# Three tiles and three loads for the normalised values of a spatial gating unit, with their operations placed behind a product of the group ahead

## The chip, the cores and the metric

The kernel runs on one core of one Trainium2 chip. The metric is device time in microseconds (us) for one launch; lower is better. Three runs of the kernel before took 1842.79, 1843.56 and 1844.47 us, so the median is 1843.56 us. Engines are named as in the profile: PE is the matrix engine (PEld its weight loads), DVE the vector engine, ACT the scalar engine, POOL GpSimd, and SP the engine whose queue issues the transfers (DMAs).

## The reference

The reference is one step of a two-layer decoder trunk over 1024 prompt tokens and 8 sample tokens, in float32. Layer 0 is a gated linear recurrence; layer 1, "layer B" here, is a chunked MLP with spatial gating. After each comes a gated per-layer embedding. The change lies in layer B:

```
def chunk_mlp_mixer(h, w_in, ln_g, ln_b, w_sp, b_sp, w_out):
    proj = h @ w_in
    u, v, z = jnp.split(proj, 3, axis=-1)
    u = jax.nn.gelu(u)
    v = layernorm(jax.nn.gelu(v), ln_g, ln_b)
    ...
    w = jnp.where(jnp.tril(jnp.ones((c, c), dtype=bool))[None], w_sp, 0.0)
    s = jnp.einsum('gts,bnsgd->bntgd', w, vc) + b_sp.T[None, None, :, :, None]
    s = s.reshape(B, n * c, D_INNER)[:, :L]
    y = (u * s * jax.nn.silu(z)) @ w_out
    v_tail = v[:, ((L - 1) // c) * c:]
    return y, v_tail
```

The inner width is 2048, in 8 groups of 256 channels; each group has its own causal 128 x 128 matrix w_sp, applied to each of the 8 chunks of 128 prompt tokens. The normalised rows of the last chunk (v_tail) are an output.

## The kernel before

Activations lie with channels on the 128 partitions and tokens along the free axis. The 1032 tokens are cut into three column chunks, called 0, 1 and 2, of 384, 384 and 264 (the last holds the 8 sample tokens); OFF, W and NT give each chunk's start, width and number of 128-token blocks (3, 3, 2). A float32 product is made from three products of split operands (`mm3`, L234 to L236): the weights are split into a high and a low part by ACT (L150) and DVE (L151), the activations likewise.

`unit` (L478) computes two output tiles of 128 channels for all three chunks. Chunks 0 and 1 together take seven products of half size instead of eight, with weights that are sums of blocks (`ssum`, split into `shi` and `slo`); chunk 2 is a plain product (`last`, x264 in the profile). The sums of the partial results are DVE operations: L520, L532, L539, L546 and L552, with ACT's copy L516 ahead of the first. Each of them reads a PSUM bank, which PE can use again once it is read. `unit` takes two callbacks: `pre(mm, c)` ahead of a product and `out(mm, c, src)` when the result of half mm and chunk c is there.

Layer B first computes v: GELU, a transposition so that tokens lie on partitions, statistics for the layer norm (L1567), and a store to DRAM, one tensor `vraw[g]` for each group of 256 channels. Then it runs over the eight groups g. A group does, in program order:

- a unit for u with GELU (`gated`, L1705);
- a load of the whole of `vraw[g]`, 1 MB, to the tile `vn` (L1722; one buffer), and eight DVE operations L1724, one for each 128-token block, that subtract the mean and multiply by the reciprocal deviation in place;
- two small loads (L1726, L1727), two POOL operations that turn the last block into the output v_tail (L1729, L1730), and its store (L1731);
- `spatial`: a unit for z. Its `pre` multiplies vn by the group's matrix (L1680, into the PSUM tile psp), adds the bias (DVE, L1683) and multiplies by u (POOL, L1689; DVE in the last group). Its `out` makes the sigmoid of z (ACT, L1695), the product sigmoid times z (DVE, L1696, the "gating product"), the product with s (DVE, L1697), and stores the result to DRAM (L1698).

In `spatial` of groups 0 to 6 the calls of `pre` come in the order (0,0), (0,2), (1,1), (0,1), (1,0), (1,2), where the first number is the half and the second the chunk. So chunk 1 of vn is read for the last time in (0,1), chunk 0 in (1,0) and chunk 2 in (1,2), which is also the last gating product of the group. In group 7 chunk 2 comes first.

In groups 4 to 7 further DVE operations (L438 to L444) and transfers prepare sums of activations for the output projection. At the end of group 7, `first_four` uses the space of vn for four results of another product: ACT copies them there (L362), and they are stored to DRAM (L363).

The order of PE's instructions is the program's own. On the other engines and on SP the compiler orders instructions by a simulated schedule of its own; `tc.high_priority` raises instructions in it (the sums of `unit` among them), and `tc.issue_after(x)` makes the instructions of a block come after x in the queue of x's engine. Each engine, and SP with its DMA issues, works through its queue in order, so an instruction that waits holds all that stand behind it. A tile with one buffer can be loaded again only when all its readers are done.

Of the kernel before, what the change touches and what calls it, by code (L numbers as in the profile page):

```python
# [8 lines left out]
F32 = mybir.dt.float32  # L9
# [4 lines left out]
ALU = mybir.AluOpType  # L14
# [3 lines left out]
P = 128  # L18
# [8 lines left out]
DV = 256  # L27
# [14 lines left out]
OFF = (0, 384, 768)  # L42
W = (384, 384, 264)
NT = (3, 3, 2)
# [37 lines left out]
def trunk_kernel(ctx, tc, xT, st, pT, nrm, wina, lbl, gna, wouta, winb, lng, lnb, lngr, lnbr,  # L82
                 wsp, bsp, woutb, wgate, wproj, cst, msk,
                 yT, so_p, so_s, cv_p, cv_s):
    nc = tc.nc
    V, A, G, PE = nc.vector, nc.scalar, nc.gpsimd, nc.tensor
# [3 lines left out]
    def pool(stack, name, bufs=1, **kw):  # L90
        return stack.enter_context(tc.tile_pool(name=name, bufs=bufs, reuse_waits="tile", **kw))
# [122 lines left out]
    def take(*key):  # L214
        n = taken[0]
        assert order[n] == key, (order[n], key)
        load(n)
        if order[n:n + 2] == [("p", 0, 1), ("oa", 0, 0)]:
            fetch_weights(n + 1)
        else:  # L220
            load(n + 1, key[0] == "b")
        taken[0] += 1
        return loaded[n]


    last, rest = {}, {}
# [143 lines left out]
    def load_zt(zt, parts, stage, n=2, lag=0, tie=True, behind=None):  # L370


        todo = [(ozd[c][:, k0 + k:k0 + k + n, :], *(x[:, k:k + n, :] for x in zt[c, k0][:2]), W[c])
                for c, k0 in parts for k in range(0, zt[c, k0][2], n)]
        return load_list(todo, stage, lag, tie, behind)
# [50 lines left out]
    def p_in_act(l, stage, load=True):  # L426

        fh, fl = (t.rearrange("p k t -> p (k t)")[:, :2 * T].rearrange("p (k t) -> p k t", k=2)
                  for t in (hh[2], hl[2]))
        for c in CH:  # L430
            o = slice(OFF[c], OFF[c] + W[c])
            for k in range(2 if load else 0):
                load_split(fh[:, k, o], fl[:, k, o], pT[l][:, k, o], stage(W[c]))
        return ([fh[:, :, OFF[c]:OFF[c] + W[c]] for c in CH], [fl[:, :, OFF[c]:OFF[c] + W[c]] for c in CH])
# [1105 lines left out]
    vraw = [dram.tile([P, 8, DV], F32, name=f"vraw{g}") for g in range(8)]  # L1540
# [50 lines left out]
    wb2 = pool(sB, "workB2", side="right")  # L1591
    wst = wb2.tile([P, 8, P], F32, name="wst")
# [23 lines left out]
    mv = wb.tile([P, 8, 2], F32, name="mv")  # L1616
    ss_ = wb2.tile([P, MI, NS], F32, name="ss_")
    ln = {}
# [47 lines left out]
    def spatial(g, vn, us, wt, then={}, early=False):  # L1666
        bts = []
        for mm in range(2):
            bt = wb2.tile([P, P], F32, name="bt", bufs=2)
            V.scalar_tensor_tensor(bt, rw[:, g, :], lg[:, 1, 2 * g + mm:2 * g + mm + 1], bspb[:, g, :],  # L1670
                                   ALU.mult, ALU.add)
            bts.append(bt)
        ss = {}

        def pre(mm, c):
            m = 2 * g + mm
            w, nt, n0 = W[c], NT[c], OFF[c] // P
            pss = p2[0].tile([P, 3, P], F32, name="psp", tag="p2", bufs=2)
            for i in range(nt):
                PE.matmul(pss[:, i, :], vn[:, n0 + i, mm * P:(mm + 1) * P], wst[:, g, :], start=True, stop=True)  # L1680
            s = ss[mm, c] = wb2.tile([P, 384], F32, name="s", bufs=3)
            with tc.high_priority(offset=PRI):
                V.scalar_tensor_tensor(s[:, :nt * P].rearrange("p (n t) -> p n t", t=P), pss[:, :nt, :],  # L1683
                                       lg[:, 0, m:m + 1],
                                       bts[mm].rearrange("p (o t) -> p o t", o=1).broadcast_to([P, nt, P]),
                                       ALU.mult, ALU.add)
            if c == 2:
                G.tensor_copy(s[:, 256:264], ln["s"][:, m, :])
            (V if g == 7 else G).tensor_tensor(s[:, :w], s[:, :w], us[mm, c][:, :w], ALU.mult)  # L1689

        def out(mm, c, src):
            w, s = W[c], ss[mm, c]
            sg = wb2.tile([P, 384], F32, name="sg", bufs=2)
            with tc.high_priority(offset=PRI if g == 7 else 0):
                A.activation(sg[:, :w], src, AF.Sigmoid)  # L1695
                V.tensor_tensor(sg[:, :w], sg[:, :w], src, ALU.mult)  # L1696
                V.tensor_tensor(s[:, :w], s[:, :w], sg[:, :w], ALU.mult)  # L1697
            nc.sync.dma_start(ozd[c][:, 2 * g + mm, :], s[:, :w])  # L1698

        unit(wt, wide_b, wb2, out, pre, early, then)  # L1700

    def gated(us):
        def out(mm, c, src):
            us[mm, c] = wide()
            A.activation(us[mm, c][:, :W[c]], src, AF.Gelu_apprx_tanh)  # L1705
        return out

    def sums_b():

        t = stats.rearrange("p n m s -> p (n m s)")  # L1710
        t = [t[:, :384], t[:, 384:]] + [wb2.tile([P, 384], F32, name=f"mix{i}") for i in range(2)]
        yield from mix_early([(tdr[3], j, 0) for j in range(4)] + [(tdr[2], j, 8) for j in range(2)], lambda: t)
        yield

    for g in range(8):
        us = {}
        if g == 4:
            sums = sums_b()
            next(sums)
        unit(take("B", 2 * g), wide_b, wb2, gated(us), then={i: lambda: next(sums) for i in ((), (3,), (3,), (3, 7))[max(g - 4, 0)]})  # L1720
        vn = wb2.tile([P, 8, DV], F32, name="vn", bufs=1)
        nc.sync.dma_start(vn, vraw[g])  # L1722
        for n in range(8):
            V.tensor_scalar(vn[:, n, :], vn[:, n, :], mv[:, n, 0:1], ln["rstd"][:, n:n + 1], ALU.subtract, ALU.mult)  # L1724
        gb = wb2.tile([P, 2, DV], F32, name="gb", bufs=1)
        nc.sync.dma_start(gb[:, 0, :], lngr[g].partition_broadcast(P))  # L1726
        nc.sync.dma_start(gb[:, 1, :], lnbr[g].partition_broadcast(P))  # L1727
        cv = gb[:, 0, :]
        G.tensor_tensor(cv, vn[:, 7, :], cv, ALU.mult)  # L1729
        G.tensor_tensor(cv, cv, gb[:, 1, :], ALU.add)  # L1730
        nc.sync.dma_start(cv_p[:, g * DV:(g + 1) * DV], cv)  # L1731
        if g < 7:
            spatial(g, vn, us, take("B", 2 * MI + 2 * g), {3: lambda: next(sums)} if g in (4, 5) else {})
        else:

            zt = {(0, 0): (hh[0], hl[0], 8), (1, 0): (*xm[1], 4), (1, 4): (*xm[0], 4), (2, 0): (hh[2], hl[2], 8)}
            ph, pl = p_in_act(1, None, False)


            free = ws[0].tile([P, 1024], F32, name="wstg3", bufs=1)  # L1740
            zq_to = itertools.cycle([free[:, 384 * i:384 * i + 384] for i in range(2)] +
                                    [t[:, 3 * i:3 * i + 3, :].rearrange("p a b -> p (a b)") for t in (rw, bspb)
                                     for i in range(2)] + [gb.rearrange("p a b -> p (a b)")[:, :384]])
            zq = load_zt(zt, [(1, 0), (0, 0), (1, 4)],
                         lambda w: next(zq_to)[:, :w].rearrange("p (k t) -> p k t", k=1),
                         1, ZQ, False)

            def fetch(n):
                return lambda: [next(zq, None) for _ in range(n)]

            pieces = [(pT[1][:, k, OFF[c]:OFF[c] + W[c]], ph[c][:, k, :], pl[c][:, k, :], W[c]) for c in CH for k in range(2)]
            pq = load_list(pieces, lambda w: ws[0].tile([P, 512], F32, name="ssum", bufs=2)[:, :w], 2, False,
                           lambda: rest["u2"])
            place = [None]
            fillb = pple(1, ph, pl, 1, lambda c, mm: place[0](c, mm))

            def both(m, n):
                def go():
                    for _ in range(m):
                        next(pq, None)  # L1760
                    fetch(n)()
                return go

            def first_four():
                vt = wb2.tile([P, 8, DV], F32, name="vn", bufs=1).rearrange("p a b -> p (a b)")
                place[0] = lambda c, mm: vt[:, 384 * mm:384 * mm + 384]
                for _ in range(4):
                    next(fillb)
                    tk.tick()

            spatial(g, vn, us, take("B", 2 * MI + 2 * g),
                    {0: both(2, ZQ), 1: lambda: next(sums), 2: both(2, 4), 3: both(2, 8), 4: both(2, 4), 8: first_four}, True)
# [155 lines left out]
```

## Time and profile before

| | us |
|---|---|
| median of the three runs | 1843.56 |
| the profiled execution | 1848.1 |
| its span, first to last instruction | 1846.4 |
| PE busy | 1821.9 |
| DVE busy | 1363.5 |
| ACT busy | 897.8 |
| POOL busy | 379.1 |

The granted clock of PE was 0.998 of full speed over the span. The groups of layer B lie between about 1195 and 1560 us. In the profile's rows, a time at the front is the start in us from the span's start, the second number the duration; "x3" counts instructions; a bracket at the end gives the idle time of the engine before the row, and what ended it. In the table of waits the three numbers are the total in us, the count and the longest. In the table of DMAs they are the size and the median time in us from issue to landing. In rows by window they are the window, its length, the busy time (and count) of PE, PEld, DVE, ACT and POOL, then PE's granted clock, the DMA engines' busy share and GB/s. The names u, c, s, sg and stats are tiles; "u" is also the name under which the sums u2 and u4 appear, and "c" stands for c22.

### The profile page before, as it was taken

How to read it: one execution, taken by the hardware profiler on the slowest of the kernel's cores; microseconds unless marked ns; L12 is line 12 of the kernel's file. 1: busy time of each engine (PE TensorE's matmuls, PEld its weight loads, DVE VectorE, ACT ScalarE, POOL GpSimd, SP SyncE). 2: the span in 40 equal slices, each digit the busy share in tenths (PEclk: the TensorE clock that was granted, in tenths of full speed). 3: DMA queues.
4: the chain of work that ended last, by engine and by line, in shares of the span. 5: the costliest groups of instructions: out<-in, count | busy, mean ns of one | idle time of the engine just before them, and what ended most of it. 6: DMA issues, size and time to landing. Idle time of an engine off the chain costs nothing.

```text
span 1846.4 us, 37297 instructions
## 1 busy us (share of the span) xinstructions
PE 1821.9 (99%) x14545; PEld 1788.9 (97%) x14545; DVE 1363.5 (74%) x2787; ACT 897.8 (49%) x1907; POOL 379.1 (21%) x384
## 2 busy tenths in 40 slices
PE   9999999999999999999999999999999999999998
PEld 8999999999999999999999999999999999999997
DVE  7866888788878886877747655587777877877654
ACT  7533366556656655354535544433333335444442
POOL 0000011111111110000424233344454550000322
PEclk9999999999999999999999999999999999999999
DMA  6233344345444357763144433333334537953222
GB/s 221 80 122 106 105 131 138 106 155 172 150 134 138 121 175 245 249 206 106 48 157 141 140 94 92 92 107 112 109 101 152 181 117 231 304 187 97 82 92 93
DMA packets 164721, 258.06 MB, mean 140 GB/s; under 512 B 16128, under 2 KB 137024, under 8 KB 163520
## 3 DMA queue, kind: packets, MB, share of 16 engines
q1 hardware_dynamic: 164544, 255.68, 43.4%
q8 instruction: 114, 1.87, 0.4%
q14 instruction: 63, 0.52, 0.1%
HBM read 182.82 MB, written 72.80 MB: 138 GB/s over the span
## 4 chain that ended last, share of the span: by engine, by line
PE 85%; DVE 7%; DMA 3%; issue 1%; ACT 1%; POOL 1%; SPq 0%; DVEq 0%; ACTq 0%; POOLq 0%
PE ps_proj L234 21%; PE ps_proj L235 20%; PE ps_proj L236 20%; PE ps_d L234 3%; PE ps_d L236 3%; PE ps_d L235 3%; PE ps_o L234 2%; PE ps_o L235 2%; PE ps_o L236 2%; PE psp L1680 1%; PE pt_o L1048 1%; DVE wlo L151 1%; PE po L236 1%; PE po L235 1%; PE po L234 1%
## 5 line engine op out<-in xcount | busy, mean ns | idle before, releaser
L234 PE MATMUL ps_proj<-bh,whi 128*128 128x384 f32 (+1 forms) x2192 | 701.1, 320 | 3.3 <-DVE vl L230 0.8
L235 PE MATMUL ps_proj<-bl,whi 128*128 128x384 f32 (+1 forms) x2192 | 682.3, 311 | 2.0 <-DVE bl L230 1.4
L236 PE MATMUL ps_proj<-bh,wlo 128*128 128x384 f32 (+1 forms) x2192 | 682.3, 311 | 0.7 <-DVE wlo L151 0.7
L234 PEld LDWEIGHTS ps_proj<-bh,whi 128*128 128x128 f32 x2192 | 412.5, 188 | 11.5 <-issue 4.3
L235 PEld LDWEIGHTS ps_proj<-bl,whi 128*128 128x128 f32 x2192 | 413.1, 188 | 4.6 <-DVE bl L230 4.5
L236 PEld LDWEIGHTS ps_proj<-bh,wlo 128*128 128x128 f32 x2192 | 411.6, 188 | 1.0 <-DVE wlo L151 1.0
L151 DVE TENSOR_TENSOR wlo<-wstg,whi 128x1024 fp32r<-128x1024 f32 x143 | 178.4, 1248 | 96.0 <-ACT whi L150 95.7
L150 ACT CAST whi<-wstg 128x1024 fp32r<-128x1024 f32 x143 | 150.1, 1049 | 144.6 <-PE ps_proj L235 122.2
L150 ACT CAST shi<-ssum 128x512 fp32r<-128x512 f32 x152 | 94.1, 622 | 190.6 <-PE ps_proj L235 90.0
L151 DVE TENSOR_TENSOR slo<-ssum,shi 128x512 fp32r<-128x512 f32 x152 | 113.5, 748 | 10.4 <-ACT shi L150 10.0
L243 POOL TENSOR_TENSOR rsq<-rms_e,mhalf 128x3 f32<-128x3 f32 x15 | 17.2, 1146 | 399.2 <-DVE rms_e L295 399.2
L1006 DVE TENSOR_TENSOR qk<-qk,t 128x384 f32<-128x384 f32 (+1 forms) x144 | 76.6, 536 | 12.0 <-PE pC L956 11.2
L234 PE MATMUL ps_proj<-xmh,shi 128*128 128x384 f32 x244 | 83.3, 341 | 2.0 <-DVE u L520 1.4
L236 PE MATMUL ps_proj<-xmh,slo 128*128 128x384 f32 x244 | 81.7, 335 | 0.0
L235 PE MATMUL ps_proj<-xml,shi 128*128 128x384 f32 x244 | 81.7, 335 | 0.0
L234 PE MATMUL ps_o<-bh,whi 128*128 128x384 f32 (+1 forms) x232 | 73.6, 317 | 0.8 <-ACT bh L392 0.5
L235 PE MATMUL ps_o<-bl,whi 128*128 128x384 f32 (+1 forms) x232 | 72.8, 314 | 0.4 <-DVE bl L396 0.4
L236 PE MATMUL ps_o<-bh,wlo 128*128 128x384 f32 (+1 forms) x232 | 72.7, 313 | 0.0
L1427 DVE TENSOR_TENSOR tmp<-tmp,pj 128x384 f32<-128x384 f32 (+1 forms) x48 | 26.5, 552 | 52.4 <-ACT tmp L1426 48.4
L270 POOL TENSOR_TENSOR ssq<-ssq,tmp 128x384 f32<-128x384 f32 (+1 forms) x36 | 34.9, 969 | 111.7 <-ACT tmp L269 111.7
L243 POOL TENSOR_TENSOR rsq<-ss_e,mhalf 128x3 f32<-128x3 f32 (+2 forms) x32 | 28.5, 889 | 140.2 <-DVE ss_e L1042 134.7
L1689 POOL TENSOR_TENSOR s<-s,u 128x384 f32<-128x384 f32 (+1 forms) x42 | 46.8, 1115 | 45.0 <-DVE s L1683 44.5
(397 smaller groups left out, 4223.6 us busy)
## 6 DMA issues: line engine op xcount, KB each, us to landing
wstg<-in_wina SPq DMA_DIRECT2D x48, 512.0 KB, 3.7
wstg<-in_winb SPq DMA_DIRECT2D x48, 512.0 KB, 3.9
pj<-ppd SPq DMA_DIRECT2D x16, 516.0 KB, 4.9
S<-in_st SPq DMA_DIRECT2D x16, 512.0 KB, 3.9
vb<-vd SPq DMA_DIRECT2D x16, 512.0 KB, 4.8
out_so_s<-S SPq DMA_DIRECT2D x16, 512.0 KB, 3.5
wstg<-in_wouta SPq DMA_DIRECT2D x16, 512.0 KB, 4.4
wstg<-in_wgate SPq DMA_DIRECT2D x16, 512.0 KB, 3.7
```

Of the source, the lines that this page charges most:

```text
L150: A.copy(hi, src)
L151: V.tensor_tensor(lo, src, hi.bitcast(F32), ALU.subtract)
L234: PE.matmul(ps, wh, xh, start=first, stop=False, skip_group_check=more)
L235: PE.matmul(ps, wh, xl, start=False, stop=False, skip_group_check=more)
L236: PE.matmul(ps, wl, xh, start=False, stop=last, skip_group_check=more)
L243: G.tensor_tensor(y, e, mhalf[:, :n], ALU.pow)
L270: eng.tensor_tensor(ssq, ssq, sq[:, :w], ALU.add)
L1006: V.tensor_tensor(lev, lev, t2.rearrange("p two (n o) -> p two n o", o=1).broadcast_to([P, 2, n, lv]), ALU.mult)
L1048: PE.transpose(pt[:, m, :], on[:, m * P:(m + 1) * P], ident)
L1427: V.tensor_tensor(gt[:, :w], gt[:, :w], pj[:, OFF[c]:OFF[c] + w], ALU.mult)
L1680: PE.matmul(pss[:, i, :], vn[:, n0 + i, mm * P:(mm + 1) * P], wst[:, g, :], start=True, stop=True)
L1689: (V if g == 7 else G).tensor_tensor(s[:, :w], s[:, :w], us[mm, c][:, :w], ALU.mult)
```

## The change

The tile vn of 8 blocks becomes three tiles, vn0, vn1 and vn2, with 3, 3 and 2 blocks, one for each chunk. Each has its own load, 384, 384 and 256 KB, written in the program in the order 1, 0, 2, and the operations L1724 of a chunk follow its load. From group 1 on, those eight operations are placed, by `issue_after`, behind the last gating product that the program has issued by then, which is that of half 1 and chunk 2 of the group ahead. `spatial` and the output v_tail read the tile of their chunk. `first_four` takes two of the tiles, two results in each, instead of the one.

```
             for i in range(nt):
-                PE.matmul(pss[:, i, :], vn[:, n0 + i, mm * P:(mm + 1) * P], wst[:, g, :], start=True, stop=True)
+                PE.matmul(pss[:, i, :], vn[c][:, i, mm * P:(mm + 1) * P], wst[:, g, :], start=True, stop=True)
...
-                V.tensor_tensor(sg[:, :w], sg[:, :w], src, ALU.mult)
+                rest["gate"] = V.tensor_tensor(sg[:, :w], sg[:, :w], src, ALU.mult)
...
-        vn = wb2.tile([P, 8, DV], F32, name="vn", bufs=1)
-        nc.sync.dma_start(vn, vraw[g])
-        for n in range(8):
-            V.tensor_scalar(vn[:, n, :], vn[:, n, :], mv[:, n, 0:1], ln["rstd"][:, n:n + 1], ALU.subtract, ALU.mult)
+        vn = [None] * 3
+        for c in (1, 0, 2):
+            vn[c] = wb2.tile([P, NT[c], DV], F32, name=f"vn{c}", bufs=1)
+            nc.sync.dma_start(vn[c], vraw[g][:, OFF[c] // P:OFF[c] // P + NT[c]])
+            for i in range(NT[c]):
+                n = OFF[c] // P + i
+                with tc.issue_after(rest["gate"].ins) if g else ExitStack():
+                    V.tensor_scalar(vn[c][:, i, :], vn[c][:, i, :], mv[:, n, 0:1], ln["rstd"][:, n:n + 1], ALU.subtract,
+                                    ALU.mult)
...
-        G.tensor_tensor(cv, vn[:, 7, :], cv, ALU.mult)
+        G.tensor_tensor(cv, vn[2][:, 1, :], cv, ALU.mult)
...
             def first_four():
-                vt = wb2.tile([P, 8, DV], F32, name="vn", bufs=1).rearrange("p a b -> p (a b)")
-                place[0] = lambda c, mm: vt[:, 384 * mm:384 * mm + 384]
+                vt = [wb2.tile([P, 3, DV], F32, name=f"vn{i}", bufs=1).rearrange("p a b -> p (a b)") for i in range(2)]
+                place[0] = lambda c, mm: vt[mm // 2][:, 384 * (mm % 2):384 * (mm % 2) + 384]
```

More of the change, by code (lines that the diff above doesn't have):

```diff
@@ L1676, in pre @@
             m = 2 * g + mm
-            w, nt, n0 = W[c], NT[c], OFF[c] // P
+            w, nt = W[c], NT[c]
             pss = p2[0].tile([P, 3, P], F32, name="psp", tag="p2", bufs=2)
             for i in range(nt):
-                PE.matmul(pss[:, i, :], vn[:, n0 + i, mm * P:(mm + 1) * P], wst[:, g, :], start=True, stop=True)
+                PE.matmul(pss[:, i, :], vn[c][:, i, mm * P:(mm + 1) * P], wst[:, g, :], start=True, stop=True)
             s = ss[mm, c] = wb2.tile([P, 384], F32, name="s", bufs=3)
```

## The prediction

> **What bounds the kernel now.** I read the profile's page first, for the busiest engine, then the waits of TensorE (PE) between 1190 and 1560 us, the stretch that holds the eight groups of layer B, and then the timelines around each wait.
>
> ```profile
> span 1846.4 us, 37297 instructions
> PE 1821.9 (99%) x14545; PEld 1788.9 (97%) x14545; DVE 1363.5 (74%) x2787; ACT 897.8 (49%) x1907; POOL 379.1 (21%) x384
> ...
> PE ps_pple L234 <- ACT vn L362: 1.4, 1, 1.4
> PE ps_proj L234 <- DVE u L520: 1.4, 2, 1.1
> PE ps_d L234 <- DVE c L539: 0.7, 1, 0.7
> PE ps_proj L234 <- ACT u L516: 0.6, 1, 0.6
> PE ps_proj L234 <- DVE sg L1696: 0.5, 1, 0.5
> ```
>
> PE is busy for 99% of the span, and the change takes no matmul away. So all it can win is idle time of PE inside the stretch where it acts, and the five rows of waits are all of that: 1.4 + 1.4 + 0.7 + 0.6 + 0.5 = 4.6 us. No weight (whi, wlo, shi, slo) is among the things PE waits for, so weights arrive early enough here.
>
> What a wait costs in pace is more than its idle time. I looked for one marker that each group has: the four matmuls L1680 of the second half's last chunk.
>
> ```profile
> 1233.18 0.60 PE L1680 MATMUL psp<-wst,vn 128*128 128x128 f32 x4
> 1279.12 0.60 PE L1680 MATMUL psp<-wst,vn 128*128 128x128 f32 x4
> 1323.92 0.60 PE L1680 MATMUL psp<-wst,vn 128*128 128x128 f32 x4
> 1368.33 0.60 PE L1680 MATMUL psp<-wst,vn 128*128 128x128 f32 x4
> 1412.74 0.60 PE L1680 MATMUL psp<-wst,vn 128*128 128x128 f32 x4
> 1459.43 0.60 PE L1680 MATMUL psp<-wst,vn 128*128 128x128 f32 x4
> 1503.84 0.60 PE L1680 MATMUL psp<-wst,vn 128*128 128x128 f32 x4
> ```
>
> These are groups 0 to 6, and from one to the next it takes 45.94, 44.80, 44.41, 44.41, 46.69 and 44.41 us. Three steps agree to the hundredth, so 44.41 us is a group in which PE never stops. The others are over it by 1.53 (into group 1), 0.39 (into group 2) and 2.28 us (into group 5).
>
> Now what causes them. VectorE (DVE), entering group 1, and PE behind it:
>
> ```profile
> 1242.82 0.42 DVE L1696 TENSOR_TENSOR sg<-sg,ps_proj 128x264 f32<-128x264 f32 x1
> 1244.50 0.41 DVE L1724 TENSOR_SCALAR vn<-vn,mv,rsq 128x256 f32<-128x256 f32 x1 [1.25 <-DMA vn<-vraw]
> 1244.83 0.43 DVE L1697 TENSOR_TENSOR s<-s,sg 128x264 f32<-128x264 f32 x1
> 1245.17 1.38 DVE L1724 TENSOR_SCALAR vn<-vn,mv,rsq 128x256 f32<-128x256 f32 x4
> 1246.46 0.55 DVE L520 TENSOR_TENSOR u<-ps_proj,u 128x384 f32<-128x384 f32 x1
> 1246.93 0.68 DVE L151 TENSOR_TENSOR slo<-ssum,shi 128x512 fp32r<-128x512 f32 x1
> 1247.53 2.04 DVE L1724 TENSOR_SCALAR vn<-vn,mv,rsq 128x256 f32<-128x256 f32 x3
> 1249.48 1.21 DVE L151 TENSOR_TENSOR wlo<-wstg,whi 128x1024 fp32r<-128x1024 f32 x1
> ...
> 1247.07 0.45 PE L234 MATMUL ps_proj<-xmh,shi 128*128 128x384 f32 x1 [0.32 <-DVE u L520]
> ```
>
> The first row is the last gating product of group 0. The first normalisation (L1724) comes right behind it in DVE's queue and holds the whole queue for 1.25 us until its load lands. The sum L520, which hands a PSUM bank back to PE, stands five normalisations further on, and PE sits idle from 1246.75 to 1247.07 for it. Entering group 5 it is the same, larger, and a second sum (L539) is still late eight microseconds on:
>
> ```profile
> 1420.20 0.42 DVE L1696 TENSOR_TENSOR sg<-sg,ps_proj 128x264 f32<-128x264 f32 x1
> 1423.90 0.42 DVE L1724 TENSOR_SCALAR vn<-vn,mv,rsq 128x256 f32<-128x256 f32 x1 [3.27 <-DMA vn<-vraw]
> ...
> 1425.87 0.54 DVE L520 TENSOR_TENSOR u<-ps_proj,u 128x384 f32<-128x384 f32 x1
> ...
> 1433.04 0.54 DVE L539 TENSOR_TENSOR c<-ps_d,u 128x384 f32<-128x384 f32 x1
> ...
> 1426.47 0.44 PE L234 MATMUL ps_proj<-xmh,shi 128*128 128x384 f32 x1 [1.07 <-DVE u L520]
> 1433.64 0.45 PE L234 MATMUL ps_d<-bh,whi 128*128 128x384 f32 x1 [0.66 <-DVE c L539]
> ```
>
> Here PE idles 1.07 + 0.66 = 1.73 us and the step is 2.28 over: a stop costs its idle time and some 0.28 us for starting again (0.55 / 2). Into group 1 the step holds two stops, this 0.32 and the 0.6 of ACT's copy L516; 1.53 less their idle 0.92 is 0.61, or 0.30 each. So the load's share there is 0.32 + 0.30 = 0.62. The copy L516 runs before any L1724 and is not touched.
>
> **The change, part by part.** *The loads.* Why does the load land late? It reads into the one tile vn, which all 16 products of the group ahead must have left, and SyncE (SP) issues in order:
>
> ```profile
> DVE vn L1724 <- DMA vn<-vraw: 10.8, 7, 3.3
> ...
> 1227.52 0.83 PE L1680 MATMUL psp<-wst,vn 128*128 128x128 f32 x6
> 1230.29 0.83 PE L1680 MATMUL psp<-wst,vn 128*128 128x128 f32 x6
> ...
> 1234.65 4.52 SPq L1698 DMA_DIRECT2D ozd<-s  x2
> 1239.27 0.38 SPq L1722 DMA_DIRECT2D vn<-vraw  x1
> ...
> 1416.65 0.38 SPq L1722 DMA_DIRECT2D vn<-vraw  x1
> ...
> vn<-vraw SPq DMA_DIRECT2D x7, 1024.0 KB, 5.4
> wstg<-in_winb SPq DMA_DIRECT2D x27, 512.0 KB, 3.7
> mix<-ozd SPq DMA_DIRECT2D x12, 192.0 KB, 3.6
> ```
>
> With three tiles, chunk 1 is free once the products at 1227.52 have read it, chunk 0 after those at 1230.29, and only chunk 2 after 1233.18. Chunk 1 can start almost 11 us and chunk 0 some 8 us before 1239.27, each behind whichever stores SP has ahead of it. The 384 KB of such a load lie between the 192 KB at 3.6 and the 512 KB at 3.7 us; I take 3.7. Even issued after 1234.65 both are there by 1239.1, ahead of the gating product's end at 1243.24. Chunk 2 leaves as now, at 1239.27, and lands by 1243.0, while its two operations come last. In group 5 both early chunks get the same lead on 1416.65, against a wait of 3.27 us. So I put DVE's seven waits, 10.8 us in all, at nothing.
>
> Should the order not change, all three staying behind the same two stores, chunk 1 would still land at 1239.27 + 3.7 = 1243.0, and the forecast would hold for group 1. In group 5 the first stop, 1.07 us, would need a landing 6.2 us after the issue instead of the 7.25 from 1416.65 to 1423.90, which three eighths of the bytes should manage. So the sum does not hang on how far ahead the loads get.
>
> The 16 further issues cost SP 16 x 0.38 = 6.1 us spread over the eight groups. Behind them in the queue stand the stores L1698, weight loads, and the staging of the last group. PE has no wait on a weight in this stretch, so a delay of 0.4 to 0.8 us is covered; without that cover it would be at most 0.8 us in each of seven groups.
>
> A larger doubt is the size. The table has 5.4 us for 1024 KB and 3.7 for 512 KB, so halving saves only a third: most of a small load is not bytes. The Trainium skill's page "DMA: Bandwidth & Descriptors", section "Bandwidth", advises batching transfers to at least 1 MiB, and its section "Anatomy of one DMA" fits, for loads issued by GpSimd, 2.0 us plus the bytes at 436 GB/s: by estimate 4.4 us for one load against 2.9 + 2.9 + 2.6 = 8.4 for three that follow one another, so that by this rule the last operations would come 4.0 us later and the sum would be a loss. The trace agrees that small loads are dear; whether they follow one another or overlap it doesn't show for these, and that is a rival below.
>
> *The tie.* It removes and adds no operation: eight of L1724 before and after. It forbids them to run ahead of the gating product; in both timelines above they already stand behind it. Its price is therefore nothing where the queue keeps its order. Queued behind them are the sum L520, the weight splits L151 and the POOL product that reads chunk 2. With the wait gone L520 ends 1.25 us earlier in group 1, at 1245.8, against the 1246.75 at which PE needs it; in group 5 3.27 earlier, at 1423.1, against 1425.40, and L539 at 1430.3, against the 1431.6 at which PE, itself 1.35 us earlier (1.07 + 0.28), would ask for it. All three stops go. What is late next in group 1 is L516's copy, which stays.
>
> *PE's waits.* Group by group PE now checks one tile; with three it may hold more checks.
>
> ```profile
> L1680 PEldq EVENT_SEMAPHORE  x7: 51/51/51, 1259.5 to 1525.7; - x7
> ```
>
> At most 14 more of 0.051 us, 0.7 us; the groups at 44.41 hold one each. I take zero, and keep 0.7 as the end.
>
> *The rest.* Group 0 has no tie and waits for the variance, not for the load; the two tiles of first_four are free at the last products, well before their copies. Both cost nothing.
>
> Sum: 0.62 + 0.39 + 2.28 = 3.29 us off the profiled execution's own 1848.1 us (span 1846.4 and 1.7 around it), that is 0.178%. The median of the runs, 1843.56, is 0.25% below that execution; the same share of it gives 1843.56 - 3.28 = 1840.3 us. A difference of 0.2%, 3.7 us, is about what a measurement of this kernel can tell from none, so the forecast is a real gain that stays just inside.
>
> **The rivals.** *More goes.* The last group's two stops (0.5 and 1.4) lie behind a chain of DVE operations, transfers and ACT copies; if the order there re-forms, they save 1.9 + 2 x 0.28 = 2.5 more: 5.8 us, 1837.8. For it: everything in DVE's queue moves forward. Against: nothing in their rows names vn's load.
>
> *Given back.* What follows the stretch is the only place where transfers fill the engines:
>
> ```profile
> 1560.00:1600.00 40.00, 39.16 (x259) 38.98 (x258) 28.13 (x54) 21.24 (x43) 0.00 (x0) 1.00 0.98 324
> ```
>
> The DMA share is 0.98. If PE arrives 3.3 us sooner but those bytes don't, it waits there: 1843.6. Against: those transfers are issued by the same progress and move with it, and PE idles only 0.84 us there.
>
> *The block in front of the sum (slower).* Once the loads are early, all eight operations are ready at the gate's end, and the scheduler may queue them, and the splits L151 (0.68 and 1.21), before L520. Eight at a third of a microsecond (1.38 / 4) are 2.8, with L1697 and L520 itself 3.7: from 1243.24 that ends at 1246.9, where PE needs it at 1246.75. The point where it decides is here: with both splits in front too, 1.9 us are added, and the stop is 2.0 + 0.28 in group 1 and, from 1420.62 (end 1426.2 against 1425.40), 0.8 + 0.28 in one like group 5. One of the first and six of the second are 8.8 us against the 3.29 removed: +5.5, or 1849.1. Against: L520 has a raised priority and now passes three of them.
>
> *One after another (slower).* If the three loads queue behind the same stores and each waits for the one ahead, at 3.7 us each chunk 0 lands at 1246.7 and chunk 2 at 1250.4. The fifth operation, in front of L520, would then end at 1247.4, and L520 at 1247.9, some 0.9 later than now; in the groups that stop already that is 2.7 us, in all seven 6.3: 1846.3 to 1849.9. This is the course that the Trainium skill's "DMA: Bandwidth & Descriptors", section "Bandwidth", with its advice to batch, would lead one to expect. Against it: the tiles come free 3 us apart (1227.52, 1230.29, 1233.18).
>
> **How the numbers follow.** The forecast's mechanism gets 0.55, of which 0.14 I put beyond 3.7 us, since 3.29 is so near it and further small stops may go. More goes: 0.15, all faster. Given back: 0.14, no change. The block: 0.12, of which 0.11 beyond 0.2%. One after another: 0.04, half of it. Faster 0.14 + 0.15 = 0.29; slower 0.11 + 0.02 = 0.13; same 0.58. The range runs from the full second case, 1837.8, to the given-back case with the scatter of the runs before (up to 1844.47), 1844.5. It leaves out the two slower rivals and a little of the second, under 0.2.
>
> **What would show it.** Right: no row in which L1724 waits for its load for over a microsecond; the steps between the markers all 44.4 but the first, at 45.3; L516's 0.6 still there. The loads right: the chunk-1 issue of group 1 by 1235. Wrong: PE waits on L520 in most groups (the block), DVE waiting in the middle of its normalisations (one after another), or all steps at 44.4 and PE idle after 1560 (given back).

## The result, and the profile after

The kernel after takes 1840.70 us (median of 17 runs, 1839.70 to 1842.35) against 1843.09 us (17 runs, 1841.96 to 1844.47): a ratio of 0.9985, with a 95% interval from 0.9978 to 0.9991. Run again beside other runs of the kernel before, it gave 0.9983 (0.9974 to 0.9992). Forecast were 1840.3 us and 0.178% less; measured are 0.15 to 0.17% less. It is faster, by less than 0.2%.

The page of the kernel after, and PE's waits between 1185 and 1560 us, all of them:

```profile
span 1839.0 us, 37343 instructions
...
PE 1819.6 (99%) x14545; PEld 1788.3 (97%) x14545; DVE 1362.3 (74%) x2787; ACT 896.7 (49%) x1907; POOL 377.3 (21%) x384
...
PE ps_proj L234 <- ACT u L516: 0.4, 1, 0.4
```

Of five rows of waits one is left, the copy L516. The markers (the products L1680 of half 1, chunk 2), groups 0, 1, 4, 5 and 6:

```profile
1232.23 0.60 PE L1680 MATMUL psp<-wst,vn 128*128 128x128 f32 x4
1277.39 0.60 PE L1680 MATMUL psp<-wst,vn 128*128 128x128 f32 x4
...
1410.63 0.60 PE L1680 MATMUL psp<-wst,vn 128*128 128x128 f32 x4
1455.04 0.60 PE L1680 MATMUL psp<-wst,vn 128*128 128x128 f32 x4
1499.45 0.60 PE L1680 MATMUL psp<-wst,vn 128*128 128x128 f32 x4
```

The steps are 45.16 us into group 1 and then 222.06 for five, or 44.41 each. Entering group 1, DVE in the kernel after (L1724 has become L1728, the load L1722 has become L1724):

```profile
1241.67 0.42 DVE L1696 TENSOR_TENSOR sg<-sg,ps_proj 128x264 f32<-128x264 f32 x1
1242.01 0.41 DVE L1728 TENSOR_SCALAR vn<-vn,mv,rsq 128x256 f32<-128x256 f32 x1
1242.34 0.43 DVE L1697 TENSOR_TENSOR s<-s,sg 128x264 f32<-128x264 f32 x1
1242.68 1.38 DVE L1728 TENSOR_SCALAR vn<-vn,mv,rsq 128x256 f32<-128x256 f32 x4
1243.97 0.55 DVE L520 TENSOR_TENSOR u<-ps_proj,u 128x384 f32<-128x384 f32 x1
```

The order is that of before, one instruction after the other; only the bracket with the wait is gone, in this and in all seven groups. The loads that did it, on SP, and their times to landing:

```profile
1230.91 0.38 SPq L1724 DMA_DIRECT2D vn<-vraw  x1
...
1233.93 0.38 SPq L1724 DMA_DIRECT2D vn<-vraw  x1
...
1238.08 0.42 SPq L1724 DMA_DIRECT2D vn<-vraw  x1
...
vn<-vraw SPq DMA_DIRECT2D x14, 384.0 KB, 4.2
vn<-vraw SPq DMA_DIRECT2D x7, 256.0 KB, 3.3
```

One number must be read with care: the spans of the two profiles differ by 1846.4 - 1839.0 = 7.4 us, three times the difference of the medians. The profiled execution of the kernel before, at 1848.1 us, was slower than each of its 17 runs. What of its waits was its own, the first experiment tells.

### The profile page after: what moved, and what is told of

It reads as the page before. It is cut to its first block, busy times and chain, and to the rows that moved or that the text cites. A ratio compares the mean times of both kernels' runs of the same rounds, so it can differ in the third digit from the quotient of the medians.

```text
span 1839.0 us, 37343 instructions
## 1 busy us (share of the span) xinstructions
PE 1819.6 (99%) x14545; PEld 1788.3 (97%) x14545; DVE 1362.3 (74%) x2787; ACT 896.7 (49%) x1907; POOL 377.3 (21%) x384
## 4 chain that ended last, share of the span: by engine, by line
PE 88%; DVE 6%; DMA 2%; ACT 1%; issue 1%; POOL 1%; SPq 0%; DVEq 0%; ACTq 0%; POOLq 0%
PE ps_proj L234 21%; PE ps_proj L235 21%; PE ps_proj L236 21%; PE ps_d L234 3%; PE ps_d L236 3%; PE ps_d L235 3%; PE ps_o L234 2%; PE ps_o L235 2%; PE ps_o L236 2%; PE psp L1680 1%; PE pt_o L1048 1%; PE po L236 1%; PE po L235 1%; PE po L234 1%; PE pt_g L1562 1%
## 5 line engine op out<-in xcount | busy, mean ns | idle before, releaser
L234 PE MATMUL ps_proj<-bh,shi 128*128 128x384 f32 x164 | 55.9, 341 | 0.0
```

The costliest lines, as they stand in the source:

```text
L234: PE.matmul(ps, wh, xh, start=first, stop=False, skip_group_check=more)
```

## The experiments

The theory: the first normalisation stands in DVE's queue ahead of the sum L520 and holds it until the load lands; the change wins by ending that wait. The rivals: the gain comes from the tie (the `issue_after`); from three tiles as such; or small loads follow one another and spoil it. All ratios are against runs of the kernel before on the same chip.

**The tie alone** (tie_only).

```
-        for n in range(8):
-            V.tensor_scalar(vn[:, n, :], ...)
+        for n in range(8):
+            with tc.issue_after(rest["gate"].ins) if g else ExitStack():
+                V.tensor_scalar(vn[:, n, :], ...)
```

> The kernel before with the tie alone: one tile, one load, the eight normalisations placed behind the gating product of the group ahead. In the kernel before they already stand behind it, so the order of every queue is the same as before. By the theory (the load's landing holds DVE's queue; the tie by itself does nothing) the ratio is 1.000, within 0.0007, and DVE waits some 10.8 us on the load in seven waits. By the rival that the tie makes the gain it would be 0.9985. It is also a second look at the kernel before: if the steps over 44.41 us into groups 1, 2 and 5 and the two stops of the last group come again, they belong to the kernel; if not, to the one execution that was profiled.

Ratio 1.000 (0.9991 to 1.0008). The tie alone does nothing, as DVE's queue keeps its order. So this profile serves as a second execution of the kernel before: PE's and DVE's waits in the stretch (DVE's on the load alone), and the markers of groups 0, 1, 2, 4 and 5:

```profile
PE ps_proj L234 <- DVE u L520: 1.3, 2, 0.9
PE ps_d L234 <- DVE c L539: 0.7, 1, 0.7
PE ps_proj L234 <- ACT u L516: 0.6, 1, 0.6
...
DVE vn L1725 <- DMA vn<-vraw: 11.0, 7, 2.7
...
1232.52 0.60 PE L1680 MATMUL psp<-wst,vn 128*128 128x128 f32 x4
1279.05 0.60 PE L1680 MATMUL psp<-wst,vn 128*128 128x128 f32 x4
1324.17 0.60 PE L1680 MATMUL psp<-wst,vn 128*128 128x128 f32 x4
...
1413.00 0.60 PE L1680 MATMUL psp<-wst,vn 128*128 128x128 f32 x4
1458.52 0.60 PE L1680 MATMUL psp<-wst,vn 128*128 128x128 f32 x4
```

The waits on L520 and L539 come again and belong to the kernel. The two stops of the last group (0.5 and 1.4) don't come each time: they are among what made the profiled execution slow, and the one behind L362 appears in other profiles too, with 0.6 us in the second one of the kernel after (after_again) and 1.4 to 1.6 in three slower kernels below (no_lead, split_no_tie and late_load). The steps are 46.53, 45.12 and 45.52, against 45.94, 44.80 and 46.69 before: each group's share varies between these two executions, the sum hardly. Against the kernel after (45.16, 44.41, 44.41) the difference is 1.37 + 0.71 + 1.11 = 3.19 us. Some 0.2 of the 1.37 belong to the copy L516, whose stop is 0.6 us here and 0.4 in the kernel after, so the load's share is about 3.0.

**Smaller loads without the lead** (one_tile).

```
-        nc.sync.dma_start(vn, vraw[g])
-        for n in range(8):
+        for c in (1, 0, 2):
+            o = slice(OFF[c] // P, OFF[c] // P + NT[c])
+            nc.sync.dma_start(vn[:, o, :], vraw[g][:, o])
+            for n in range(o.start, o.stop):
...
```

> Three loads (384, 384, 256 KB) with the tie, but into slices of the one tile, so that all three go out behind the last reader, where the one load went. It has the smaller loads without the lead. If smaller pieces suffice (the first 384 KB land 1.5 to 2 us sooner than 1024 KB), DVE's wait on the first load falls from 10.8 to some 3 us and the ratio is 0.9985 to 0.9992. If the lead is what counts, DVE still waits 8 us or more and the ratio is 0.9995 to 1.0005. If three loads follow one another, the wait moves to the middle of the normalisations and the ratio is over 1.001.

Ratio 0.9985 (0.9976 to 0.9994), the whole gain. SP's loads, and DVE's wait:

```profile
1237.94 0.88 SPq L1724 DMA_DIRECT2D vn<-vraw  x2
1240.47 0.32 SPq L1698 DMA_DIRECT2D ozd<-s  x1
1240.83 0.43 SPq L1724 DMA_DIRECT2D vn<-vraw  x1
...
DVE vn L1727 <- DMA vn<-vraw: 2.5, 3, 1.4
```

The first two loads go out where the one load went, the third one store later, and still the wait falls from 11.0 to 2.5 us, and PE's waits on L520 and L539 are gone. Three tiles, and with them the head start, are not needed; two pieces of 384 KB that land sooner are enough, since the five operations ahead of L520 use only these.

**Three tiles without the lead** (no_lead).

```
+        for c in (2, 1, 0):
+            vn[c] = wb2.tile([P, NT[c], DV], F32, name=f"vn{c}", bufs=1)
+            with tc.issue_after(rest["ld"].ins) if c < 2 else ExitStack():
+                rest["ld"] = nc.sync.dma_start(vn[c], vraw[g][:, OFF[c] // P:OFF[c] // P + NT[c]])
         for c in (1, 0, 2):
...
```

> Three tiles and the tie as after, but chunk 2 is loaded first and the other two behind it on SP, so that the tiles that come free early are not loaded early. The third load even stands behind one more store than the one load did. By the theory DVE waits on chunk 1 and again on chunk 0, both in front of the sum L520: at least the 10.8 us of before, and a ratio of 1.000 to 1.003. If three tiles were the gain by themselves (releases, fewer dependencies), it would be 0.9985.

Ratio 1.0061 (1.0048 to 1.0074): the direction was right, the price too small by half, as 1.003 was the most that I expected. DVE and PE entering group 1, and the totals:

```profile
1245.67 0.73 DVE L1730 TENSOR_SCALAR vn<-vn,mv,rsq 128x256 f32<-128x256 f32 x2 [2.65 <-DMA vn<-vraw]
1246.32 0.55 DVE L520 TENSOR_TENSOR u<-ps_proj,u 128x384 f32<-128x384 f32 x1
...
1246.93 0.69 PE L234 MATMUL ps_proj<-xmh,shi 128*128 128x384 f32 x1 [2.19 <-DVE u L520]
...
PE ps_proj L234 <- DVE u L520: 5.9, 6, 2.2
...
DVE vn L1730 <- DMA vn<-vraw: 19.5, 14, 2.7
```

The load of chunk 0 stands last on SP, behind a further store, while its operations stand ahead of L520. The same tiles with the loads in another order lose 11 us where the kernel after wins 3: it is the time at which the operations ahead of the sum can run that decides, not the tiles. The one stop of 2.19 us lengthened its step by 4.0 (the last section shows why); between this profile and that of tie_only, 6.6 us lie between the markers of groups 0 and 6 and 5.4 behind the last of them.

**After without the tie** (no_tie).

```
-                with tc.issue_after(rest["gate"].ins) if g else ExitStack():
-                    V.tensor_scalar(vn[c][:, i, :], ...)
+                V.tensor_scalar(vn[c][:, i, :], ...)
```

> After without the tie: three tiles, three early loads. The scheduler then puts three of the eight normalisations in among the gating operations of the group ahead and the other five right ahead of the split that follows them, all before the gating product. By the theory they are then again at the head of DVE's queue before their loads land (the loads go out at the same place, some 4 us before): DVE waits 5 us or more in all, in the part where it is busiest, and the ratio is 0.9990 to 1.003. By the rival that early loads alone make the gain and the tie is idle, DVE waits under 2 us and the ratio is 0.9985 or lower.

Ratio 1.0038 (1.0026 to 1.0051), above the 1.003 that I gave as the end, and half of my reason for it was wrong. DVE before the last gating product of group 1, PE behind it, and the totals:

```profile
1287.01 1.69 DVE L1727 TENSOR_SCALAR vn<-vn,mv,rsq 128x256 f32<-128x256 f32 x5
1288.63 1.21 DVE L151 TENSOR_TENSOR wlo<-wstg,whi 128x1024 fp32r<-128x1024 f32 x1
1289.76 0.41 DVE L1696 TENSOR_TENSOR sg<-sg,ps_proj 128x264 f32<-128x264 f32 x1
...
1290.23 0.39 PE L234 MATMUL ps_proj<-bh,whi 128*128 128x264 f32 x1 [0.90 <-DVE sg L1696]
...
PE ps_proj L234 <- DVE sg L1696: 6.6, 7, 1.1
...
DVE vn L1727 <- DMA vn<-vraw: 0.2, 1, 0.2
```

The loads come in time (0.2 us of waiting, where I expected 5), but the eight operations now stand ahead of the gating product, which also hands a bank back. Their work alone makes it late, and PE waits 6.6 us in seven groups. So the tie, worth nothing beside the late load, is worth the difference of 0.9985 and 1.0038, some 10 us, beside early ones.

**Smaller loads without the tie** (split_no_tie): one_tile with the `issue_after` taken out.

> One tile, three loads, no tie. The scheduler then puts two of the eight normalisations in front of the weight split and of the last gating product, the other six behind. Without the tie and with eight in front the run with three tiles lost 7 us, and PE waited for the gating product, not for the load. Two in front are 0.7 us of work, but the first of them must wait for a load that lands about 4 us after 1238, near the gating product's own time of 1241.5: PE waits on L1696 in most of seven groups for 0.3 to 1 us, and the ratio is 1.000 to 1.004. If the smaller loads make the gain whatever the order, it is 0.9985.

Ratio 1.0034 (1.0022 to 1.0047), within the range, by both ways at once:

```profile
PE ps_proj L234 <- DVE sg L1696: 3.9, 6, 1.4
...
DVE vn L1726 <- DMA vn<-vraw: 10.0, 7, 1.8
```

Two operations ahead of the gating product hold it until the load lands. No load was issued earlier here; three smaller ones were enough for the scheduler to move these two forward.

**The place in the queue alone** (hold): one tile, one load.

```
-            rest["sum"] = V.tensor_tensor(u2, ps[:, :384], u2, ALU.add)
+            rest["sum"] = rest["first"] = V.tensor_tensor(u2, ps[:, :384], u2, ALU.add)
...
         for n in range(8):
+            with tc.issue_after(rest["first"].ins):
...
```

> The kernel before, one tile and one 1 MB load, but the eight normalisations placed behind the sum L520 of the group's own first unit, which stood between the fifth and the sixth of them. Nothing is loaded sooner or in smaller pieces. If the cost is the place in DVE's queue (the sum that frees the bank behind an operation that waits for the load), PE's two waits on L520 (1.3 to 1.4 us) go, the load's wait comes 1.4 us of work later and shrinks from 11 to some 3 us, and the ratio is 0.9982 to 0.9992. If the landing itself is what costs, it only moves to the sums L532 and L539 and the ratio is 0.9995 or more.

Ratio 0.9985 (0.9976 to 0.9994), the same gain with nothing loaded otherwise. DVE entering group 1, and its wait on the load:

```profile
1241.55 0.55 DVE L520 TENSOR_TENSOR u<-ps_proj,u 128x384 f32<-128x384 f32 x1
1242.02 0.68 DVE L151 TENSOR_TENSOR slo<-ssum,shi 128x512 fp32r<-128x512 f32 x1
1242.62 3.65 DVE L1725 TENSOR_SCALAR vn<-vn,mv,rsq 128x256 f32<-128x256 f32 x8
...
DVE vn L1725 <- DMA vn<-vraw: 0.8, 2, 0.6
```

The sum goes first, and behind it and a split even the 1 MB load is nearly always there: DVE's wait falls from 11.0 to 0.8 us. So neither a smaller load nor an earlier one is needed for the gain. What this run doesn't tell apart is the place of the sum and the shorter wait that comes with it, since the operations are reached later; the next run lengthens the wait at this place.

**The wait doubled, behind the sum** (late_load): the kernel before with `issue_after` of the store of half 1, chunk 0 around the load. The scheduler then puts the operations behind L520 by itself, as in hold.

> The same order on DVE as in the run that holds the normalisations behind L520, but the one load goes out a store later (behind the store of half 1, chunk 0), some 2.5 us later. It doubles the suspected wait behind the sum: DVE waits 15 to 20 us in seven waits, the sums L532 and L539 come late, and PE stops at L539 in most groups. Theory: ratio 1.001 to 1.006. If PE has slack enough there, so that only L520 matters, it is 0.9985 as without the delay.

Ratio 1.0017 (1.0008 to 1.0026). The longest wait, into group 2, another into group 4, PE behind the longest, and the total:

```profile
1292.97 2.68 DVE L1727 TENSOR_SCALAR vn<-vn,mv,rsq 128x256 f32<-128x256 f32 x8 [5.82 <-DMA vn<-vraw]
1382.73 2.68 DVE L1727 TENSOR_SCALAR vn<-vn,mv,rsq 128x256 f32<-128x256 f32 x8 [2.98 <-DMA vn<-vraw]
...
1298.44 0.44 PE L234 MATMUL ps_d<-bh,whi 128*128 128x384 f32 x1 [1.86 <-DVE c L539]
...
DVE vn L1727 <- DMA vn<-vraw: 21.5, 7, 5.8
```

DVE waits 21.5 us, twice as long as in the kernel before. The loss is some 3 us against that kernel, and 6.3 against hold (medians of 1846.75 and 1840.49 us), which has this order almost without the wait (0.8 us). PE stops at L539 twice (2.4 us), not in most groups as I expected. By the steps, the waits of 2.75 and 2.98 us into groups 3 and 4 cost PE nothing (44.42 and 44.41 us); the 5.82 us cost 3.77, the shorter waits into groups 5 and 6, where L438 to L444 share DVE, 0.82 and 0.43, and the 2.65 us into group 1 some 0.25. Ahead of the sum, in the two profiles of the kernel before, waits of up to 1.59 us into groups 3, 4 and 6 cost nothing either; but 1.25 and 1.84 us into group 1 cost 0.62 and 1.20, and 3.27 and 2.11 into group 5 cost 2.28 and 1.11. So a wait behind the sum isn't free: it has more slack before PE notices. This profile is of the slowest of the eleven runs, so part of its stops can be its own.

**Eight loads** (eight_loads): after with a load for each block.

> After with a load for each 128-token block: 3, 3 and 2 loads of 128 KB in the places of the three, 40 more in all. If small loads follow one another, or their fixed part fills the queue, the last block lands late, DVE waits in the middle of the normalisations and the ratio is 1.000 or more. If they overlap, as the loads one behind the other in the run with one tile did, DVE waits under 2 us, and the ratio is 0.9985, at most 0.0003 worse for two further microseconds of SP in each group.

Ratio 0.9983 (0.9974 to 0.9992). DVE waits for none of them; in the table of DMAs:

```profile
vn<-vraw SPq DMA_DIRECT2D x56, 128.0 KB, 3.3
```

128 KB land in 3.3 us, 384 KB in 4.2 and 1024 KB (before) in 5.4, so by estimate from these three some 3.0 us of a load don't depend on its size. Loads in flight together share that part: SP issues the first three of group 1 within 1.33 us. The Trainium skill's advice to batch to 1 MiB ("DMA: Bandwidth & Descriptors", section "Bandwidth") shows no effect here, where the steps are 44.41 us with either size; as a reason against this change it failed.

**Both cures** (after_hold: after, with the operations placed behind L520 as in hold), and **the kernel after again** (after_again).

> After (three tiles, three early loads) with the normalisations placed behind the sum L520 instead of the gating product: both cures together. By the theory each of them alone already takes away every stop that the load causes, so together they give no more: ratio 0.9980 to 0.9988, the same as after within 0.0005, steps of 44.41 but for some 45.1 into group 1, where PE waits for ACT's copy L516. If a wait were left that the steps do not show, it would be under 0.9978.

> The kernel after, unchanged, beside the same runs of the kernel before. What is open is the size: the steps between the markers add up to 3.2 to 3.4 us (0.18%), the measured ratio is 0.9985 with an interval that reaches from 0.9978 to 0.9991. If the steps tell it all, the ratio is 0.9980 to 0.9985 and the steps are 45.1 once and 44.41 five times again; if something of the gain is given back after the stretch, the steps are the same and the ratio is 0.9986 to 0.9990.

0.9979 (0.9970 to 0.9988) and 0.9983 (0.9974 to 0.9992), with medians of 1840.90 and 1840.66 us: no difference between the two that these runs can tell. The second profile of the kernel after has steps of 45.30 and five times 44.41. With one_tile, hold and eight_loads there are five kernels that gain the same, and none clearly more.

## Why the prediction was right

**The bound and the sum.** Each of the three stops named (L520 into group 1, L520 and L539 into group 5) is gone, and the steps but the first are 44.41 us. For the 0.39 us of group 2 no stop was named, and the table of waits has none; the rows show PE idle for 0.11 us ahead of the first product behind L520 (from 1291.78 to 1291.89), and the second execution has a wait of 0.45 on L520 there. The sum of 3.29 us stands against 3.0 to 3.2 between two executions and 0.15 to 0.17% (2.4 to 3.2 us) in the ratios. That counting steps between markers gave more than PE's idle time (0.32 + 1.07 + 0.66 = 2.05 us) was right: the stops cost about half as much again as the rows of waits say.

**Its terms.** I took 0.62, 0.39 and 2.28 for groups 1, 2 and 5; the second execution, reckoned the same way, has 1.20, 0.71 and 1.11. The large one belonged to a landing of 7.25 us that does not come each time. That the sum was so near is partly luck: these shifts cancel.

**The loads.** Chunk 1 goes out at 1230.91, before the 1235 that I set as a mark. I took 3.7 us to landing for the pieces; they took 4.2 and 3.3. That the sum does not hang on the head start was argued and has now been shown (one_tile). The head start with one whole load (a second buffer for vn) was not run.

**The tie.** "Its price is therefore nothing where the queue keeps its order" held; but I never asked what the queue would do without it. It would not have kept its order, and the change would have lost some 7 us. The point I missed is that the scheduler answers an early or a smaller load by moving the operations forward.

**The rivals.** *More goes*: the last group's two stops are gone from the profile after, but also from the second profile of the kernel before, and the ratio has no room for 5.8 us. *Given back*: nothing that the profiles show. From the marker of group 6 to the end of the span it is 339.55 and 339.62 us in the two profiles of the kernel after, and 339.57 in the second one of the kernel before. *The block in front of the sum*: it did not happen, but without the tie a block ahead of another bank's release did, at a cost near what such a thing was reckoned at (+5.5 us forecast for the one, 7 us measured for the other). *One after another*: eight loads took no harm; the no_lead order shows the price where a load is last on SP and its operations first on DVE.

**PE's checks.** Zero was right: stall-free steps are 44.41 us in both kernels, although the products L1680 of the kernel after have 22 checks where those of the kernel before have 7: 15 more, where I took 14 as the most.

## What to carry to other kernels

When a busy engine shows a few stops, look at the queue of the engine that should have freed its bank: an operation that waits for a transfer costs what stands behind it, and putting the bank's release ahead of it (one `issue_after`) can do as much as loading sooner or in pieces. When loads are made earlier or smaller, pin the operations that use them as well, since the scheduler will otherwise move them in front of work that is due. Count pace between markers, as idle time alone leaves part of each stop out, and profile the kernel before twice before believing in a single stop.

## What was not expected of the hardware

A short stop of PE costs about 0.28 us beyond its idle time (into group 5 of the kernel before: 1.73 us idle in two stops, the step 2.28 over). The rows show where it goes. Ahead of that group's first stop products start some 0.12 us apart, but each is shown as 0.28 long, so idle time counted from the shown end leaves out 0.16; and the second product behind the stop starts 0.27 us after the first, where 0.17 is usual.

The two longest stops in the steps cost far more: 1.86 us in late_load lengthened its step by 3.77, and 2.19 in no_lead by 4.0. Behind them PE's granted clock was halved for a while, which it was not behind the 1.43 us of split_no_tie. In rows by window, where the third number from the end is the granted clock:

```profile
1246.90:1248.90 2.00, 1.97 (x6) 1.97 (x7) 2.00 (x3) 0.00 (x0) 1.35 (x1) 0.50 0.06 20
1248.90:1250.90 2.00, 2.00 (x9) 2.00 (x9) 1.68 (x4) 0.17 (x1) 1.45 (x2) 0.65 0.00 0
...
1300.40:1302.40 2.00, 2.00 (x10) 2.00 (x9) 1.25 (x2) 0.96 (x3) 0.00 (x0) 0.50 0.24 70
...
1243.70:1245.70 2.00, 1.94 (x16) 1.95 (x17) 2.00 (x8) 0.00 (x0) 0.00 (x0) 1.00 0.67 171
```

The first two are no_lead behind its 2.19 us, the third is late_load, the last split_no_tie. In no_lead each of the ten products behind the stop is followed 0.32 us later or more, against the usual 0.17 (its first row above is 0.69 long, against 0.45 in the kernel before). So a stop of 2 us cost about twice its length here, and the price of a wait is not in proportion to it.

And 56 loads of 128 KB in place of the kernel after's 21 larger ones, in the groups 1 to 7, changed nothing measurable, though each takes 3.3 us to land.
